# Two more chunks of the output projection as filler in attention, and a final pass over two chunks with its weights in the shared buffers

## The chip, the cores and the metric

The kernel runs on one core of a Trainium2 chip. The metric is the device time of one execution in microseconds (us). TensorE (PE in the profile) multiplies, VectorE (DVE), ScalarE (ACT) and GpSimd (POOL) work elementwise, SyncE (SP) issues most DMAs. Each engine works through its own queue in order.

## What is computed

Two layers of a hybrid block run over 128 context tokens and 512 latent tokens of width 1024. The part that matters here, cut from the reference:

```python
ya = diff_attention(a_q, a_k, a_v, lam)                      # 4 heads, 256 features
yb = gqa_attention(b_q, b_k, b_v).reshape(b, L, W_B)         # 4 heads, 256 features
yc, ssd_state = ssd_mixer(...)                               # 256 features
yd, s5_state = s5_mixer(...)                                 # 256 features
y = jnp.concatenate([ya, yb, yc, yd], axis=-1) @ P['w_out']  # 1024 x 1024
x = x + gate1 * rmsnorm(y, P['g_post1'])
h = rmsnorm(x, P['g_pre2']) * (1.0 + scale2) + shift2
g, v = jnp.split(dwconv(h @ P['w_up'], P['ffn_conv_w'], P['ffn_conv_b']), 2, axis=-1)
x = x + gate2 * rmsnorm((jax.nn.silu(g) * v) @ P['w_down'], P['g_post2'])
```

## The kernel before

Activations lie with features on the 128 partitions and the 642 token columns (512 latent, 2 padding, 128 context) along the free axis. So a vector of 1024 features is 8 tiles, the chunks 0 to 7 of `self.h`. Chunks 0 to 3 hold the outputs of attention, 4 and 5 that of the SSD, 6 and 7 that of the S5. Every number that is multiplied is split into a high and a low part (`hh` and `hl`, `wh` and `wl` in the trace), and a product is three matmuls: high by high, high by low, low by high.

The columns are worked in two spans, `SPANS`: 0 to 256 and 256 to 642. One output tile of `w_out` over one span is, for each chunk, three matmuls of 256 or 386 columns, which accumulate in one PSUM bank; the bank is then copied or added into the SBUF tile `y[m]` (lines 1565 and 1567).

The order of the work follows from priorities: `self.prio(p)` gives the instructions traced in it a number, counting up, and a planner with a model of the chip's times orders each engine's queue by it; a lower number goes first where several are ready. Inside a layer the S5 comes first (0), then its GLU (10000), attention (20000), the SSD (30000), the projections (40000), all plus 100000. What comes later is filler for the gaps of these: the adaLN matmuls of layer 0 (`fill`, 160000 and 161000), then the output projection in three steps: chunks 6 and 7 from `WP[0]` (161000), chunks 0 and 1 from `WP[1]` (162000), and the final pass over chunks 4, 5, 2 and 3 with `PR["wg"]` (165000) for the first span and `PR["norm"]` (300000) for the second.

The SSD and attention run beside each other. Attention has six units; units 0 to 2 fill chunks 0 and 1, units 3 and 4 chunk 2, the last unit chunk 3. A unit handles single tiles of 128 queries: scores on PE into bank `e`, maxima on DVE, exponentials on ACT, then transposes and the products with the values on PE.

The final pass is the part after attention that all else waits for. For each span it sums the squares of `y`, and `norms` makes the norm, the gated residual, the second norm's sums and its scaling (`postnorm`, `rstd`, `prenorm`). The first span's `prenorm` is held back as `self.pending` and run in the middle of the second span's pass (`between`). Then `ffn_first` multiplies the first eight tiles of `w_up`.

Weights come through the pool `wp`, which has two raw buffers `wr` and two pairs `wh`, `wl`. `load_w` loads a tile of 512 KB into `wr`, casts it on ACT to `wh` and subtracts on DVE and POOL in turn for `wl` (lines 96 and 99). With `keep` the pair lies in another pool instead: for the final pass the pool `wo`, with four pairs `kh`, `kl`, opened on the right side behind `x`. `w_out_load(l, k0, nk)` with `nk = 2` makes two loads of two chunks by four output tiles, with `nk = 1` one load of one chunk by eight. `leading`, which `ffn_first` calls, loads the first two `w_up` tiles into `wh`, `wl` of `wp`, the next two by `load_w2` into tiles of the pool `f`, whose space attention holds until its end, and four more into the pool `wx`, which lies where `wo` was.

Of the kernel before, what the change touches and what calls it, by code (L numbers as in the profile page):

```python
# [18 lines left out]
NS = 512  # L19
PO = 514  # L20
SPLIT = 256
WG = (((4, 2), (2, 1), (3, 1)),)
WB = ("pe", "pe")
AHEAD = 1
L0BANKS = "ppvue"
WR = 2
# [47 lines left out]
class K:  # L74
# [1406 lines left out]
    def mixer(self, l, base, fill):  # L1481

        self.qd = {}
        with ExitStack() as left, ExitStack() as early:
            if l == 0:
                self.start()
            self.vec = self.vecs[l]
            self.dbg(f"h{l}", self.h[0][0].bitcast(F32))
            kq = left.enter_context(self.pool(f"kq{l}"))
            at = left.enter_context(self.pool(f"at{l}"))  # L1490
            vt = left.enter_context(self.pool(f"vt{l}"))
            proj = left.enter_context(ExitStack())
            pb = proj.enter_context(self.pool(f"pj{l}"))
            with self.pool(f"ld{l}", bufs=2) as lead, self.prio(base + PR["proj"]):
                raw = self.first_proj(l, pb, lead)
            pc = proj.enter_context(self.pool(f"pc{l}"))
            qk = early.enter_context(self.pool(f"qk{l}", "right"))
            with self.prio(base + PR["proj"]):
                sp = early.enter_context(self.pool(f"s5{l}", "right"))
                raws = {"aq0": raw[0], "ak0": raw[1]}  # L1500
                self.cf = {}
                for op in ORD.split():
                    o, n = op[0], op[1:]
                    if o == "R":
                        self.ropes(qk, int(n))
                    elif o == "V":
                        self.vdt(l, vt)
                    elif o == "P":
                        raws[n] = self.raw_proj(l, pb, n)
                    elif o == "Q":  # L1510
                        self.qk_prep(l, qk, n, raws.pop(n))
                    elif o == "C":
                        self.ssd_proj(l, pb, pc, n)
                    elif o == "Z":
                        self.proj(l, f"cz{n}", self.putcz[int(n)])
                    else:
                        for t in self.cz:
                            self.silu2(self.raw(pb), t, t)
            with self.prio(base + PR["st"]):
                self.ssd_steps(pb)  # L1520
            with self.prio(base + PR["s5"]):
                ys = self.s5(l, sp, pb)
            fill(0, base + PR["f0"])
            with self.prio(base + PR["glu"]):
                self.s5_glu(l, sp, ys)
            early.close()
            yp = self.right.enter_context(self.pool(f"y{l}", "right"))
            with self.pool(f"sd{l}", "right") as sd, self.prio(base + PR["ssd"]):
                self.ssd(l, sd, pb)
            proj.close()  # L1530
            with self.prio(base + PR["attn"]):
                self.attention(l, at, kq)
        y = [yp.tile([P, TW], F32, tag=f"y{c}", name=f"y{c}") for c in range(8)]
        with self.prio(base + WP[0]):
            self.w_out(l, y, self.w_out_load(l, 6, 2))
        fill(1, base + PR["f1"])
        with self.prio(base + WP[1]):
            self.w_out(l, y, self.w_out_load(l, 0, 2))
        return yp, y
# [58 lines left out]
    def run(self):  # L1598
        nc, tc, a, o = self.nc, self.tc, self.a, self.o
        PS = bass.MemoryType.PSUM  # L1600
        self.left0 = ExitStack()
        with self.pool("cp") as self.cp, self.pool("modp", bufs=2) as self.modp, \
                self.pool("hp") as self.hp, self.pool("wp", bufs=2) as self.wp, \
                self.pool("pd", space=PS) as self.psd, \
                tc.tile_pool(name="dp", bufs=2, space=bass.MemoryType.DRAM) as self.dp:
            self.mod, self.vecs, self.s5d = {}, {}, {}
            self.h = []
            for c in range(8):
                self.h.append(tuple(self.hp.tile([P, TW], F32R, tag=f"{q}{c}", name=f"h{q}{c}") for q in "hl"))
                for t in self.h[c]:  # L1610
                    nc.gpsimd.memset(t[:, NS:PO].bitcast(F32), 0.0)
            self.cst = self.cp.tile([P, NCST - 128], F32, tag="cst", name="cst")
            self.identr = self.cp.tile([P, 128], F32R, tag="idr", name="identr")
            xd = a["xT"]
            for l in range(L):
                base = 1000000 * l
                with ExitStack() as self.right:
                    with self.pool(f"pm{l}", space=PS) as self.psm:

                        def fill(i, p):  # L1620
                            if l == 0:
                                with self.prio(p):
                                    self.weave(self.adaln(0, 1 + i, 2 + i, self.wp))
                        yp, y = self.mixer(l, base + 100000, fill)
                        for c in range(8):
                            self.dbg(f"yc{l}{c}", self.h[c][0].bitcast(F32))
                        xp = self.right.enter_context(self.pool(f"x{l}", "right"))
                        fp = self.right.enter_context(self.pool(f"f{l}"))
                        with self.prio(base + PR["norm"]), self.pool(f"wo{l}", "right", 4) as wo:
                            self.x = [xp.tile([P, TW], F32, tag=f"x{c}", name="x") for c in range(8)]  # L1630
                            for c in range(8):
                                nc.sync.dma_start(self.x[c], xd[:, c, :])
                            ws = [sum((self.w_out_load(l, k, n, wo) for k, n in g), []) for g in WG]
                            for gi, (t0, t1) in enumerate(SPANS):
                                st = self.sums("vd"[gi])

                                def put(m):
                                    self.square(fp, st, gi, y[m], m)
                                if gi == 0:
                                    for i, w in enumerate(ws):  # L1640
                                        with self.prio(base + PR["wg"] + 1000 * i):
                                            self.w_out(l, y, w, ((t0, t1),), put if i == len(WG) - 1 else None, WB[i])
                                else:
                                    self.w_out(l, y, sum(ws, []), ((t0, t1),), put, WB[-1])
                                self.norms(fp, gi, st, y, (l, 0), (l, 1))
                        with self.prio(base + PR["first"]):
                            first = self.ffn_first(l, fp, yp)
                    self.dbg(f"xm{l}", self.x[0])
                    last = l == L - 1
                    xt = o["yT"] if last else self.dp.tile([P, 8, TW], F32, tag="xd", name="xd")  # L1650
                    with self.prio(base + 320000), self.pool(f"qb{l}", bufs=2, space=PS) as self.pbig:

                        def tables():
                            if not last:
                                with self.pool(f"t{l + 1}", "right") as tp, self.prio(base + 320300):
                                    self.s5_tables(l + 1, tp, "dd", base + 320300)
                                self.vec = self.vecs[l]

                        def finish(gi, st, y):
                            self.norms(fp, gi, st, y, (l, 1), None if last else (l + 1, 0), xt)  # L1660
                        side = ExitStack()
                        wm = None if last else side.enter_context(self.pool(f"wm{l}", "right"))

                        def other():
                            if not last:
                                yield from self.adaln(l + 1, 0, 3, wm, "vu", 3)
                        self.ffn(l, fp, yp, first, tables, finish, other(), side.close)
                    xd = xt
# [145 lines left out]
```

## Time and profile before

| | us |
|---|---|
| three runs: median | 2218.14 |
| three runs: lowest and highest | 2208.99, 2224.91 |
| the profiled execution | 2229.98 |
| its span, from the first to the last instruction | 2228.2 |

The profiled execution is 11.8 us above the median of the runs. Durations below come from it. In its trace a matmul's duration is longer than the distance to the next one, as matmuls are pipelined: the distance is what counts. In names of tiles `psp` is PSUM bank `p`, `pse` bank `e`, and so on; `kh` and `kl` are the weights of the final pass, of the `w_up` tiles 4 to 7 and of the last `w_down` tiles.

### The profile page before, as it was taken

What the parts mean: (1) busy time and instruction counts of PE and PEld (TensorE: products, weight loads), DVE (VectorE), ACT (ScalarE), POOL (GpSimd) and SP (SyncE); (2) the same over time, 40 slices, a digit from 0 to 9 for tenths busy, and PEclk for the clock granted to TensorE, in tenths of its full rate; (3) what the DMA queues carried; (4) which work ended last, traced back from release to release, by engine and by line L of the source; (5) the groups of instructions that cost most, each with busy time, mean ns of one, the idle gap of its engine ahead of it and who ended that gap; (6) DMA issues with size and microseconds to landing.
All of it is one profiled execution on the core that took longest, in us unless ns stands there. A gap on an engine that the chain in (4) does not pass through costs nothing. (4 is left out here: it accounts for less than half of the span.)

```text
span 2228.2 us, 33233 instructions
## 1 busy us (share of the span) xinstructions
PE 1970.5 (88%) x12812; PEld 1794.6 (81%) x12812; DVE 1234.3 (55%) x2847; ACT 802.3 (36%) x1614; POOL 674.9 (30%) x723
## 2 busy tenths in 40 slices
PE   5996789958889999999998888787787999999997
PEld 2895765646888878899988887776777999999996
DVE  6876885356569567233357576563845641333345
ACT  3423354334344223222334244352533442323231
POOL 3552423111143343122234332323202332222232
PEclk9996789887889999999998878877857999999998
DMA  7464325241214575422233632210102112222221
GB/s 290 134 207 155 114 89 167 84 127 47 67 39 138 159 264 169 131 82 61 88 93 93 217 117 80 84 65 10 59 19 85 39 48 86 71 73 72 80 86 48
DMA packets 93511, 230.29 MB, mean 103 GB/s; under 512 B 17960, under 2 KB 30888, under 8 KB 93352
## 3 DMA queue, kind: packets, MB, share of 16 engines
q1 hardware_dynamic: 82856, 213.46, 30.3%
q10 hardware_dynamic: 10496, 14.71, 1.9%
q8 instruction: 101, 1.65, 0.3%
q14 instruction: 58, 0.48, 0.1%
HBM read 192.21 MB, written 35.92 MB: 102 GB/s over the span
## 5 line engine op out<-in xcount | busy, mean ns | idle before, releaser
L82 PE MATMUL psb<-hh,wh 128*128 128x256 f32 (+1 forms) x1152 | 358.8, 311 | 2.3 <-DVE cv L452 2.3
L82 PE MATMUL psb<-hl,wh 128*128 128x256 f32 (+1 forms) x1152 | 358.0, 311 | 0.0
L82 PE MATMUL psb<-hh,wl 128*128 128x256 f32 (+1 forms) x1152 | 357.1, 310 | 0.0
L99 POOL TENSOR_TENSOR wl<-wr,wh 128x1024 fp32r<-128x1024 f32 (+3 forms) x83 | 182.1, 2194 | 512.2 <-ACT wh L96 488.8
L96 ACT CAST wh<-wr 128x1024 fp32r<-128x1024 f32 (+3 forms) x166 | 160.4, 966 | 420.7 <-PE psb L82 289.2
L82 PEld LDWEIGHTS psb<-hh,wh 128*128 128x128 f32 x1152 | 217.7, 189 | 13.3 <-issue 8.2
L82 PEld LDWEIGHTS psb<-hl,wh 128*128 128x128 f32 x1152 | 218.5, 190 | 3.4 <-issue 3.4
L82 PEld LDWEIGHTS psb<-hh,wl 128*128 128x128 f32 x1152 | 217.8, 189 | 3.4 <-issue 3.4
L82 PE MATMUL psp<-hh,wh 128*128 128x386 f32 (+1 forms) x544 | 182.1, 335 | 29.0 <-ACT wh L96 17.0
L99 DVE TENSOR_TENSOR wl<-wr,wh 128x1024 fp32r<-128x1024 f32 (+3 forms) x83 | 96.8, 1167 | 160.0 <-ACT wh L96 159.7
L82 PE MATMUL psp<-hl,wh 128*128 128x386 f32 (+1 forms) x544 | 177.5, 326 | 0.0
L82 PE MATMUL psp<-hh,wl 128*128 128x256 f32 (+1 forms) x544 | 175.1, 322 | 0.0
L82 PE MATMUL psb<-uh,wh 128*128 128x256 f32 (+1 forms) x544 | 169.7, 312 | 0.0
L82 PE MATMUL psb<-ul,wh 128*128 128x256 f32 (+1 forms) x544 | 169.3, 311 | 0.0
L82 PE MATMUL psb<-uh,wl 128*128 128x256 f32 (+1 forms) x544 | 168.9, 311 | 0.0
L82 PE MATMUL pse<-k,q 96*128 96x128 f32 (+5 forms) x288 | 114.5, 462 | 45.5 <-ACT at_p L1196 18.6
L82 PEld LDWEIGHTS psp<-hh,wh 128*128 128x128 f32 x544 | 109.9, 202 | 34.1 <-ACT wh L96 17.2
L82 PEld LDWEIGHTS pse<-k,q 96*128 96x128 f32 (+2 forms) x288 | 63.0, 237 | 77.4 <-issue 28.8
L1420 POOL TENSOR_TENSOR cv<-cv,cv 128x642 f32<-128x642 f32 x44 | 71.6, 1629 | 170.3 <-DVE cv L452 140.9
L451 DVE SCALAR_TENSOR_TENSOR cv<-psb,vec,cv 128x641 f32<-128x641 f32 x72 | 63.5, 882 | 103.5 <-ACT cv L450 103.5
L82 PEld LDWEIGHTS psp<-hl,wh 128*128 128x128 f32 x544 | 109.4, 201 | 2.3 <-issue 1.0
L82 PEld LDWEIGHTS psp<-hh,wl 128*128 128x128 f32 x544 | 108.5, 200 | 0.9 <-DVE wl L99 0.3
(525 smaller groups left out, 4922.6 us busy)
## 6 DMA issues: line engine op xcount, KB each, us to landing
wm<-in_w_mod SPq DMA_DIRECT2D x96, 512.0 KB
wr<-in_w_up SPq DMA_DIRECT2D x88, 512.0 KB
wr<-in_w_in SPq DMA_DIRECT2D x30, 512.0 KB
wr<-in_w_down SPq DMA_DIRECT2D x32, 384.0 KB
wr<-in_w_down SPq DMA_DIRECT2D x32, 320.0 KB
wr<-in_w_out SPq DMA_DIRECT2D x16, 512.0 KB
s_tb<-s5td SPq DMA_DIRECT2D x8, 992.0 KB
s_to<-s5td SPq DMA_DIRECT2D x8, 768.0 KB
```

The source lines that it names most:

```text
L82: self.nc.tensor.matmul(out, w, x, start=start, stop=stop)
L96: nc.scalar.copy(hv, rv)
L99: e.tensor_sub(lv, rv, hv.bitcast(F32))
L451: nc.vector.scalar_tensor_tensor(out[:, 1:TW], x[:, 0:TW - 1], w[:, 0:1], out[:, 1:TW], op0=ALU.mult, op1=ALU.add)
L1420: G.tensor_mul(cv[0], cv[0], cv[1])
```

## The change

`WG` and the pool `wo` go. Chunks 4 and 5 leave the final pass and become a second filler with priority `WP[0]`, traced behind chunks 6 and 7 and ahead of chunks 0 and 1; their tiles are added into `y`. The final pass covers chunks 2 and 3. Its two weight loads no longer use a pool of their own but the pairs `wh`, `wl` of `wp`, and they get the priority `PR["wg"]` instead of `PR["norm"]`, ahead of the loads of `x`. The first span's pass has `PR["wg"] + 1000`.

```diff
-WG = (((4, 2), (2, 1), (3, 1)),)
-WB = ("pe", "pe")
+WB = "pe"
...
         with self.prio(base + WP[0]):
-            self.w_out(l, y, self.w_out_load(l, 6, 2))
+            for k in (6, 4):
+                self.w_out(l, y, self.w_out_load(l, k, 2))
         fill(1, base + PR["f1"])
...
-                        with self.prio(base + PR["norm"]), self.pool(f"wo{l}", "right", 4) as wo:
+                        with self.prio(base + PR["norm"]):
+                            with self.prio(base + PR["wg"]):
+                                ws = self.w_out_load(l, 2, 1) + self.w_out_load(l, 3, 1)
                             self.x = [xp.tile([P, TW], F32, tag=f"x{c}", name="x") for c in range(8)]
                             for c in range(8):
                                 nc.sync.dma_start(self.x[c], xd[:, c, :])
-                            ws = [sum((self.w_out_load(l, k, n, wo) for k, n in g), []) for g in WG]
                             for gi, (t0, t1) in enumerate(SPANS):
                                 st = self.sums("vd"[gi])
...
-                                if gi == 0:
-                                    for i, w in enumerate(ws):
-                                        with self.prio(base + PR["wg"] + 1000 * i):
-                                            self.w_out(l, y, w, ((t0, t1),), put if i == len(WG) - 1 else None, WB[i])
-                                else:
-                                    self.w_out(l, y, sum(ws, []), ((t0, t1),), put, WB[-1])
+                                with self.prio(base + PR["wg"] + 1000) if gi == 0 else ExitStack():
+                                    self.w_out(l, y, ws, ((t0, t1),), put, WB)
                                 self.norms(fp, gi, st, y, (l, 0), (l, 1))
```

## Rows read from the trace of the kernel before

**Rows 1.** The page, part 1: busy us of each engine, share, instructions

```profile
PE 1970.5 (88%) x12812; PEld 1794.6 (81%) x12812; DVE 1234.3 (55%) x2847; ACT 802.3 (36%) x1614; POOL 674.9 (30%) x723
```

**Rows 2.** Stretches: length; busy PE, PEld, DVE, ACT, POOL (counts); clock, DMA share, GB/s

```profile
460.00:545.00 85.00, 55.23 (x294) 44.13 (x293) 47.95 (x123) 34.83 (x96) 16.88 (x11) 0.78 0.27 82
545.00:582.00 37.00, 33.19 (x162) 27.84 (x162) 14.21 (x37) 12.06 (x36) 0.00 (x0) 0.64 0.22 72
1570.00:1645.00 75.00, 59.51 (x291) 48.61 (x291) 53.46 (x137) 37.78 (x107) 14.34 (x11) 0.70 0.17 58
1645.00:1687.00 42.00, 38.15 (x161) 33.84 (x161) 14.00 (x35) 12.12 (x34) 0.00 (x0) 0.50 0.19 63
```

**Rows 3.** Tile `y`, by form: durations in ns (least, median, most), first and last start

```profile
L1567 DVE TENSOR_TENSOR y<-y,psp x48: 401/480/559, 492.2 to 1713.2; 128x256 f32<-128x256 f32 x24, 128x386 f32<-128x386 f32 x24
L1567 DVE TENSOR_TENSOR y<-y,pse x16: 414/482/558, 585.0 to 1714.5; 128x256 f32<-128x256 f32 x8, 128x386 f32<-128x386 f32 x8
```

**Rows 4.** Timeline of PE, layer 0, early matmuls of the final pass: start, duration

```profile
516.87 0.28 PE L82 MATMUL psp<-hh,kh 128*128 128x256 f32 x1
516.99 0.28 PE L82 MATMUL psp<-hl,kh 128*128 128x256 f32 x1
...
555.67 0.58 PE L82 MATMUL pse<-hh,kh 128*128 128x256 f32 x1
```

**Rows 5.** Timeline of PE, layer 0, final pass to `ffn_first`

```profile
581.93 0.58 PE L82 MATMUL psp<-hh,kh 128*128 128x256 f32 x1 [0.46 <-ACT hh L156]
...
590.67 0.34 PE L82 MATMUL psp<-hh,kh 128*128 128x386 f32 x1
...
600.50 0.61 PE L82 MATMUL psv<-identr,rq_y 128*128 128x128 f32 x4
...
608.39 0.34 PE L82 MATMUL pse<-hh,kl 128*128 128x386 f32 x1
...
621.00 0.58 PE L82 MATMUL psp<-hh,wh 128*128 128x256 f32 x1 [2.41 <-ACT hh L375]
```

**Rows 6.** Chain of work that ended last, layer 1, in order of time

```profile
1660.74 1.92 PE pse L82 x9
...
1667.61 1.92 PE pse L82 x9
...
1686.85 0.58 PE psp L82
...
1706.08 0.46 PE psv L82 x4
```

**Rows 7.** Timeline of DVE and then POOL, layer 0, final pass and norm

```profile
582.72 1.28 DVE L112 TENSOR_TENSOR ul<-wr,uh 128x640 fp32r<-128x640 f32 x2
...
601.15 1.66 DVE L392 SCALAR_TENSOR_TENSOR nt<-y,gpost,psv 128x256 f32<-128x256 f32 x4 [0.77 <-PE psv L82]
...
609.62 0.42 DVE L321 TENSOR_TENSOR nsq<-nsq 128x256 f32<-128x256 f32 x1
...
610.86 1.22 DVE L99 TENSOR_TENSOR kl<-wr,kh 128x1024 fp32r<-128x1024 f32 x1 [0.29 <-ACT kh L96]
612.00 2.63 DVE L318 TENSOR_TENSOR nsq<-nsq 128x256 f32<-128x256 f32 x1
...
611.85 2.50 POOL L99 TENSOR_TENSOR kl<-wr,kh 128x1024 fp32r<-128x1024 f32 x1 [3.00 <-ACT kh L96]
```

**Rows 8.** Timeline of SP and ACT, layer 0: loads of `w_out` and the wait

```profile
466.67 33.72 SPq L89 DMA_DIRECT2D wr<-in_w_out  x6
...
485.75 1.04 ACT L96 CAST wh<-wr 128x1024 fp32r<-128x1024 f32 x1 [18.25 <-DMA wr<-in_w_out]
```

**Rows 9.** Chunks 4, 5, then 1 complete: timeline (layer 0); 4, 5: tile `hl` (layer 1)

```profile
446.54 1.69 DVE L157 TENSOR_TENSOR hl<-cf,hh 128x512 fp32r<-128x512 f32 x4
...
455.12 0.28 DVE L157 TENSOR_TENSOR hl<-psd,hh 128x128 fp32r<-128x128 f32 x1
...
L157 DVE TENSOR_TENSOR hl<-cf,hh x4: 286/486/687, 1566.0 to 1568.8; 128x512 fp32r<-128x512 f32 x2, 128x128 fp32r<-128x128 f32 x2
```

## The prediction

> **What bounds the kernel now.** I read the page first. The reader should see that TensorE (PE) is busy for 88% of the span, with the other engines at 55% and less [rows 1]: a PE matter, but only where PE sets the end. So the second view is the table by stretch around the place of the change, for both layers [rows 2]. In the attention stage behind the SSD, PE is busy 55.2 of 85 us in layer 0 and 59.5 of 75 us in layer 1, DVE 48 and 53.5: no engine is full, waits between engines set the pace. In the tail of attention (its last unit) PE is busy 33.2 of 37 and 38.2 of 42 us at a granted clock of 0.64 and 0.50, and the chain of waits runs over PE without a break; there PE is the bound. The third view is PE's timeline of the final pass [rows 5]. In layer 0 its first span (256 columns) takes 581.93 to 590.67, its second (386 columns) 590.67 to 608.73. Then PE stands until the norm chain gives `ffn_first` its input at 621.00. The second span's pass is cover for that chain, not the bound. So the pass behind attention is worth much less than its matmuls, and the question is what its halves cost where they go.
>
> **How many matmuls move.** Per layer the final pass has 8 tiles x 2 spans x 4 chunks x 3 = 192 matmuls, afterwards 96: 48 of 256 columns, 48 of 386. But the trace shows that 36 of the old ones run before attention ends [rows 4]: 12 from 516.87 (two tiles' chunks 4, 5 in bank p), 6 once chunk 2 is there, 18 in bank e from 555.67 on (two tiles' chunks 4, 5, 2; two groups of nine like that). Layer 1 has the same 36. 60 of the first span's 96 are left for behind attention.
>
> **(a) First span of the final pass: -2.8 us a layer.** Of the new 48, chunk 2's matmuls for the four tiles that have a bank can go early as now, 12; 36 are left instead of 60. A 256-column matmul starts 0.12 us after the last one at full clock (516.87, 516.99 [rows 4]) and 0.213 us at the half level (1.92 us for 9 [rows 6]). 60 x 0.118 = 7.1, so 1.7 of the 8.74 us are the half-clock start; 36 x 0.118 + 1.7 = 5.9. Gain 2.8; bounds 2.8 and 8.74 x 24/60 = 3.5.
>
> **(b) Early matmuls in the tail of attention: -2 us.** Of the 18 in bank e, 12 are of chunks 4 and 5 and go. They run at half clock, and in layer 1 both groups of nine stand in the chain that ends last, 1.92 us each [rows 6]. 12 x 0.213 = 2.6 us at most, 0 if a wait shows up behind them; I take 2, since PE's pieces follow one another there.
>
> **(c) Norm sums get through PE sooner: -3 us.** The first span's column sums and its spread factor are queued on PE among the second span's matmuls: the spread stands at 600.50, 9.8 us into the second span [rows 5], some 56 matmuls of 0.176 us; in layer 1 the same spread is reached over pieces of the second span in the chain [rows 6]. With groups of 6 instead of 12, 28 of them go: 4.9 us. The other bound is 0, as the place is fixed by when DVE has the sums. I take 3.
>
> **(d) Splits of the first `w_up` tiles move into the norm chain: +5 us.** This is the hidden price. Pool `wo` goes, so chunks 2 and 3 sit in the only two `wh`/`wl` pairs of `wp` until the second span's last matmul. `leading` splits its first two tiles into these same pairs, and both `wr` buffers hold their raw data meanwhile, so tiles 2 and 3 can't even be loaded. Before, tiles 0 and 1 were split during attention and tiles 2 and 3 at 582 (DVE's two subtractions for one tile take 1.28 us at 582.72), only tiles 4 to 7 in the chain [rows 7]. Afterwards all eight are split between the end of the pass and `ffn_first`. What one batch costs there can be read: at 610.86 DVE spends 1.22 us on tile 4, and the sum of squares behind it takes 2.63 us, where its sisters take 0.42, while POOL's 2.50 us on tile 5 run beside it: 1.22 + 2.21 = 3.4. From the spread on DVE hardly rests (postnorm begins at 601.15), so tiles 0 and 1 cost another 3.4 and tiles 2 and 3 2 x 1.28 = 2.6: 6.0, less one `y` addition of 0.54 that is now over earlier. I take 5; bounds 0 (if the splits fall ahead of the spread) and 6. The loads themselves I take as hidden: the first matmul of tile 4 is needed 4 x 24 x 0.118 = 11 us behind the first of tile 0, and the cover for them is `ffn_first` itself.
> [...]
>
> **(e) Attention stage: +4 us.** 96 matmuls of chunks 4 and 5 come in, 12 of them were there already: 36 x 0.118 + 48 x 0.176 = 12.7 us of PE at full clock, and 16 more additions into `y` of 0.48 us on DVE [rows 3], 7.7 us (64 such additions become 96 in all). They can start at once: `hl` of the SSD is complete at 448 in layer 0 and 1569 in layer 1, chunk 1 at 455 in layer 0 [rows 9]. They are queued ahead of `w_out(0, 2)`, which waits for the `wh` pairs and for `y`, and behind them on PE, DVE and ACT stand the scores, maxima and exponentials of attention. PE has 29.8 us idle in layer 0, but 18.25 of these are one wait: ACT, in order, stands at the split of the `w_out` weights until 485.75 for a load issued behind 466.67 [rows 8]. I expect this wait again, since the new chunk's loads take the same place behind the adaLN loads. So some 12 us are usable, 15.5 in layer 1, against 12.7 needed: it fits barely. Nothing on the path would be 0; everything on it 12.7. Were the matmuls evenly spread (about a fifth of the time), some 40 PE steps of attention would each meet half a group of six (0.5 us) one time in five, 4 us; I take 4.
>
> No other DMA is added (eight `w_out` loads a layer before and after), the queue of SP keeps its order, and the `x` loads move behind two weight loads that are issued long before; I cost that at nothing.
>
> **Sum.** -2.8 - 2 - 3 + 5 + 4 = +1.2 us a layer, +2.4 for two. The profiled execution took 2229.98 us (span 2228.2), so 2232.4 by it; it lies 11.8 above the median of the runs, so on the median 2218.14 + 2.4 = 2220.5. I forecast 2220: no change.
>
> **Rivals.** *Cover for free* (faster): the fillers fall into idle time wholly (e = 0), and the splits ahead of the spread (d = 0), with b = 2.6 and c = 4.9: -10.3 a layer, 2218 - 20.6 = 2197. For it: idle time is there in both stages. Against it: it needs all four at once.
> *The stage is full* (slower): once the added 12.7 us exceed the idle time that attention's waits can spare, each matmul is on the path: e = 12.7, the rest as above: +9.9 a layer, 2238. For it: 12 us usable against 12.7 in layer 0. Against it: layer 1 has 15.5.
> *The order slips*: `w_out(0, 2)` is delayed by the chunk ahead of it into the last unit, where PE is the bound at half clock. If its last two tiles (24 matmuls) fall there, that is 24 x 0.213 = 5 us a layer more, 2230. Against it: in layer 0 its bank is free for the final pass at 516.87 [rows 4], 28 us before that tail.
> [...]
> [...]
>
> **How the numbers follow.** Chances: forecast 0.57, own range 2209 to 2231; cover for free 0.14; stage full 0.17; order slips 0.08; clock 0.04. About 1% is what a measurement of this kernel can tell from no change; the three runs before spread over 0.7%. Faster by over 1% (below 2196) is the clock, or free cover and a little more: 0.10. Slower by over 1% (above 2240) needs the full stage and a wait besides: 0.12. Within: 0.78. Range for 8 in 10: 2195 to 2241.
>
> **What would show it.** In the profile after: (a) attention's end to the start of the second span near 6 us instead of 8.7; (b) six instead of eighteen matmuls in bank e before it; (c) spread some 7 us behind the second span's start; (d) splits of eight `w_up` tiles between the pass and `ffn_first`, and PE's idle stretch there grown from 12 to about 23 us; (e) the stretch from the SSD's end to the last unit some 4 us longer in each layer, the 18 us wait of ACT still there. The forecast is wrong if that wait vanishes or a second one like it appears, or if the stage stretches by more than 10 us.

## The result, and the profile after

The changed kernel takes 2192.66 us (median of 4, 2190.0 to 2200.85) against 2217.89 (2208.99 to 2224.91): a ratio of 0.9895, 95% interval 0.985 to 0.9939. Measured a second time, beside the experiments, the same kernel gave 0.9884 (0.9841 to 0.9927). I had forecast no change, 2220, with 2195 as the lower end of the range. The profiled execution took 2191.5 us (span 2189.7), against 2229.98 before. The latter lies 11.8 above its median, so of the 38 us between the two traces some 12 are that one execution's.

The first view is a table of stretches in the two traces. Its marks are the ends of the last writes into tiles `hl` (S5's output, the SSD's output, each unit of attention, the norm's output).

| stretch (us) | layer 0 before | after | layer 1 before | after |
|---|---|---|---|---|
| S5's output to SSD's output | 121.6 | 115.0 | 117.1 | 117.2 |
| SSD to the end of the last unit but one | 97.6 | **77.3** | 75.8 | 75.6 |
| last unit of attention | 37.0 | 36.3 | 42.7 | 38.6 |
| final pass and norm chain | 80.6 | 78.3 | 77.8 | 76.0 |
| S5 stage of layer 1 (ahead of its SSD) | | | 240.1 | 239.9 |

27 of the 38 us are gone in layer 0 between S5 and the last unit but one; layer 1, with the same moved matmuls, gives 6. That speaks against the moved matmuls as what pays; the experiments test it.

Page, part 1, after (answers [rows 1]): PE's share is one point higher, its busy time 14 us lower.

```profile
PE 1956.1 (89%) x12812; PEld 1786.6 (82%) x12812; DVE 1245.6 (57%) x2879; ACT 802.4 (37%) x1614; POOL 676.4 (31%) x723
```

Busy time by stretch (columns as in [rows 2]). First the kernel before, from the SSD's end in layer 0, and its last unit; then after: the same two stretches of layer 0, and both in layer 1.

```profile
448.00:546.00 98.00, 65.20 (x345) 49.22 (x345) 56.28 (x148) 39.69 (x110) 17.89 (x12) 0.80 0.32 94
546.00:583.00 37.00, 33.19 (x165) 28.41 (x165) 14.21 (x37) 12.85 (x36) 0.00 (x0) 0.64 0.22 72
```
```profile
440.00:517.00 77.00, 71.03 (x359) 47.74 (x358) 47.68 (x137) 32.83 (x103) 7.74 (x8) 0.83 0.37 118
517.00:554.00 37.00, 36.76 (x253) 33.67 (x253) 24.03 (x60) 15.14 (x36) 4.14 (x2) 0.93 0.40 129
...
1537.00:1612.00 75.00, 66.42 (x380) 58.67 (x378) 58.03 (x153) 35.33 (x105) 12.45 (x10) 0.84 0.14 44
1612.00:1651.00 39.00, 35.01 (x152) 30.78 (x152) 15.17 (x38) 12.07 (x33) 0.00 (x0) 0.54 0.20 68
```

In layer 0 PE rests 6 of 77 us after, against 33 of 98 before. And the last unit now holds 253 matmuls instead of 165 in the same 37 us, at a granted clock of 0.93 instead of 0.64.

Timeline of SP after, layer 0 (answers [rows 8]):

```profile
378.94 4.16 SPq L88 DMA_DIRECT2D wr<-in_w_out  x2
403.70 18.15 SPq L226 DMA_DIRECT2D wm<-in_w_mod  x2
446.27 0.54 SPq L1182 DMA_DIRECT2D q<-d_bq  x1
449.80 0.52 SPq L1174 DMA_DIRECT2D k<-d_bk  x1
450.38 1.39 SPq L1175 DMA_DIRECT2D k<-d_bk  x1
451.82 0.65 SPq L1182 DMA_DIRECT2D q<-d_bq  x1
469.53 34.59 SPq L226 DMA_DIRECT2D wm<-in_w_mod  x14
510.52 14.26 SPq L88 DMA_DIRECT2D wr<-in_w_out  x4
```

The loads for chunks 4, 5 are issued at 378.94, before the 16 adaLN loads (`wm`) of `fill(1)` and 67 us before the q and k loads. Before, all these 16 ran first, then q and k, and the next `w_out` loads stood right behind these, at 466.67 [rows 8]. ACT's casts of weights from 375 to 540, grouped, with what ended its idle time before them:

```profile
L95 ACT CAST wh<-wr x7: 1037/1046/1050, 375.3 to 534.1; 128x1024 fp32r<-128x1024 f32 x7
...
  DMA wr<-in_w_out: 4.9, 2
```

The one wait of 18.25 us [rows 8] is gone: 4.9 us in two are left.

### The profile page after: what moved, and what is told of

It is laid out like the page before. It is cut to its first block, busy times and chain, and to the rows that moved or that the text cites. A ratio compares the mean times of both kernels' runs of the same rounds, so it can differ in the third digit from the quotient of the medians.

```text
span 2189.7 us, 33260 instructions
## 1 busy us (share of the span) xinstructions
PE 1956.1 (89%) x12812; PEld 1786.6 (82%) x12812; DVE 1245.6 (57%) x2879; ACT 802.4 (37%) x1614; POOL 676.4 (31%) x723
## 4 chain that ended last, share of the span: by engine, by line
PE 67%; DVE 15%; DMA 9%; ACT 3%; issue 2%; POOL 2%; SPq 1%; ACTq 0%; POOLq 0%; DVEq 0%
PE psb L81 34%; PE psp L81 12%; PE psd L81 7%; PE pse L81 6%; PE psv L81 5%; DMA s_tb<-s5td 2%; DMA wm<-in_w_mod 1%; DVE nt L391 1%; PE psu L1209 1%; DMA wr<-in_w_down 1%; DVE x L394 1%; DMA ck<-in_cache_ak 1%; DVE wl L98 1%; DMA q<-d_bq 1%; DVE at_s L1279 1%
## 5 line engine op out<-in xcount | busy, mean ns | idle before, releaser
L98 POOL TENSOR_TENSOR wl<-wr,wh 128x1024 fp32r<-128x1024 f32 (+3 forms) x87 | 192.3, 2211 | 502.7 <-ACT wh L95 451.6
L95 ACT CAST wh<-wr 128x1024 fp32r<-128x1024 f32 (+3 forms) x174 | 168.6, 970 | 417.9 <-PE psb L81 283.4
L81 PE MATMUL psp<-hh,wh 128*128 128x386 f32 (+1 forms) x640 | 215.3, 337 | 10.7 <-ACT hh L374 7.8
L81 PE MATMUL psp<-hl,wh 128*128 128x386 f32 (+1 forms) x640 | 209.8, 328 | 0.1
L81 PE MATMUL psp<-hh,wl 128*128 128x386 f32 (+1 forms) x640 | 207.0, 324 | 0.3 <-POOL wl L98 0.3
L81 PE MATMUL pse<-k,q 96*128 96x128 f32 (+5 forms) x288 | 107.1, 436 | 44.6 <-ACT at_p L1195 15.1
L81 PEld LDWEIGHTS psp<-hh,wh 128*128 128x128 f32 x640 | 129.0, 202 | 17.4 <-ACT hh L374 8.8
L81 PEld LDWEIGHTS psp<-hl,wh 128*128 128x128 f32 x640 | 129.3, 202 | 2.6 <-issue 1.1
L81 PEld LDWEIGHTS psp<-hh,wl 128*128 128x128 f32 x640 | 128.6, 201 | 1.4 <-issue 0.5
```

The lines of the kernel that those rows point to most:

```text
L81: self.nc.tensor.matmul(out, w, x, start=start, stop=stop)
L95: nc.scalar.copy(hv, rv)
L98: e.tensor_sub(lv, rv, hv.bitcast(F32))
```

## The experiments

Theories. *Order*: layer 0 gains because the adaLN filler is held behind the new chunks, and so the order of loads on SP changes. *Cover*: it gains because the chunks' matmuls fill idle time. One table holds the stretches of the profiled kernels, one execution of each; a ratio is the time against the kernel before, measured beside the run. Where an expectation is in us, the ratio times the 2218 of the first comparison stands beside it.

| kernel (us) | SSD, layer 0 | to last unit but one | last unit | S5 stage, layer 1 | last unit, layer 1 |
|---|---|---|---|---|---|
| before | 121.6 | 97.6 | 37.0 | 240.1 | 42.7 |
| after | 115.0 | 77.3 | 36.3 | 239.9 | 38.6 |
| after_again | 115.6 | 80.8 | 35.7 | 244.0 | 40.2 |
| fill_between | 120.5 | 98.1 | 38.5 | 250.2 | 38.5 |
| fill_last | 116.5 | 78.9 | 48.1 | 245.5 | 41.2 |
| loads_early | 118.3 | 94.6 | 42.7 | 251.7 | 28.6 |
| layer1_only | 120.6 | 101.4 | 31.6 | 242.1 | 38.6 |
| qk_rows | 120.9 | 89.6 | 31.7 | 225.5 | 42.7 |
| fill_between_rows | 121.7 | 86.9 | 38.5 | 244.8 | 38.7 |
| after_qk_rows | 113.7 | 82.6 | 34.1 | 232.7 | 38.6 |
| after_qk_rows2 | 114.4 | 83.1 | 36.8 | 230.7 | 38.5 |
| all_rows | 114.9 | 74.5 | 40.2 | 203.4 | 38.6 |
| own_pairs | 114.2 | 83.0 | 35.8 | 242.4 | 40.2 |
| rows_own_pairs | 114.7 | 82.4 | 38.9 | 237.3 | 38.6 |

**fill_between: the changed kernel with the filler where I had assumed it.**

```
         with self.prio(base + WP[0]):
-            for k in (6, 4):
-                self.w_out(l, y, self.w_out_load(l, k, 2))
+            self.w_out(l, y, self.w_out_load(l, 6, 2))
         fill(1, base + PR["f1"])
+        with self.prio(base + WP[0] + 500):
+            self.w_out(l, y, self.w_out_load(l, 4, 2))
```

> The changed kernel with one thing put back: the adaLN filler is called between chunks 6, 7 and chunks 4, 5, as my forecast had assumed it would run, so that the 16 adaLN weight loads and the q and k loads of the last attention heads stand ahead of the loads for chunks 4, 5 on SP again. All matmuls of chunks 4, 5 stay in the attention stage and the final pass keeps two chunks. Order theory (layer 0 gains because the filler is held behind the new chunk, which moves the w_out loads ahead of the q and k loads): ACT waits 15 to 18 us for w_out weights in layer 0 again, the stage from the SSD's end to the last unit is back near 90 us from 69, and the time is 2207 to 2215. Cover theory (layer 0 gains because the chunks' matmuls fill idle time): no such wait decides, 2190 to 2197.

Measured: 2231.55, ratio 1.0024 (0.9987 to 1.006): the gain is gone. By the ratio that is 2223, above both of my ranges. The waits of its attention stage in layer 0 (engine, line, waited for: us in total, times, longest) and its SP timeline:

```profile
ACT wh L95 <- DMA wr<-in_w_out: 18.7, 2, 18.4
...
PE psp L81 <- ACT wh L95: 15.9, 1, 15.9
```
```profile
467.60 0.52 SPq L1182 DMA_DIRECT2D q<-d_bq  x1
468.21 24.09 SPq L88 DMA_DIRECT2D wr<-in_w_out  x4
```

The load for chunks 4, 5 stands right behind q and k, and the wait is back with 18.4 us. Order is borne out; cover is not. But the sum of the run is not all order: layer 0, from S5's output to the norm's end, is 1 us longer than before, layer 1 behind its S5 stage some 4 us shorter, and 10 us more come from the S5 stage of layer 1. There the planner wrote another order on SP, with four q loads at 1232.15 ahead of S5's table, whose load is issued at 1249.55, 34 us into the stage; before, it goes out at 1222.07, 10 us in. That this order is the reason isn't shown: in loads_early that stage is as long (251.7) with the table's load 10 us in.

**after_again, layer1_only: the change again, and in layer 1 alone** (layer 0 keeps the code of before).

> The changed kernel itself, beside the others on one chip. Every theory: ratio 0.985 to 0.994 to before, as the first comparison gave.

> The change in layer 1 alone; layer 0 is that of the kernel before. Layer 1 has no adaLN filler and no late w_out load. Order theory: only the small terms of the forecast are left, layer 1 from the SSD's end to the end of the norm chain gets 3 to 8 us shorter and layer 0 keeps its wait of 18 us, ratio 0.996 to 0.999. Cover theory (the two layers gain alike): half of the gain, ratio 0.993 to 0.996.

Measured: 2197.45, ratio 0.9884 (0.9841 to 0.9927), and 2220.96, ratio 0.9984 (0.9954 to 1.0014). Layer 1 alone gives nothing that can be told from no change, as order expects and cover (0.993 to 0.996) does not; its trace is 3 us shorter from the SSD to the norm's end. Its layer 0 is that of the kernel before, and shows how far one code's stretches lie apart: 101.4 and 31.6 us where the trace of before has 97.6 and 37.0.

**fill_last: the kernel before with the filler called behind chunks 0, 1.** No matmul leaves the final pass.

```
-        fill(1, base + PR["f1"])
         with self.prio(base + WP[1]):
             self.w_out(l, y, self.w_out_load(l, 0, 2))
+        fill(1, base + PR["f1"])
```

> The kernel before with one thing moved: the adaLN filler is called behind w_out of chunks 0, 1 instead of ahead of it. No matmul moves between the attention stage and the final pass, which keeps four chunks. Order theory: the loads for chunks 0, 1 come ahead of the q and k loads, ACT's wait of 18.25 us is gone, the SSD ends some 4 us sooner, 2192 to 2202. Cover theory: 2214 to 2222, as before.

Measured: 2207.48, ratio 0.993 (0.9899 to 0.996), by the ratio 2202: the upper end of the range I gave for order, and well below cover's. The loads for chunks 0, 1 are issued at 382.14, ahead of the 16 adaLN loads from 403.42 on. The SSD and the stage behind it are as short as in the changed kernel, 116.5 and 78.9. But the last unit takes 48.1:

```profile
520.00:568.00 48.00, 42.97 (x201) 32.88 (x200) 21.21 (x44) 19.38 (x42) 7.16 (x3) 0.61 0.44 142
```

201 matmuls at a clock of 0.61: the end of the filler (its last matmul starts at 533.27) now lies in the stretch where PE is the bound. 24 us are gained ahead, 11 given back.

**loads_early: the kernel before, loads for chunks 0, 1 ahead of the filler, their matmuls behind it.**

```
             self.w_out(l, y, self.w_out_load(l, 6, 2))
+            w01 = self.w_out_load(l, 0, 2)
         fill(1, base + PR["f1"])
         with self.prio(base + WP[1]):
-            self.w_out(l, y, self.w_out_load(l, 0, 2))
+            self.w_out(l, y, w01)
```

> The kernel before with only the loads (and splits) for chunks 0, 1 issued right behind those of chunks 6, 7; the filler is still called ahead of the matmuls of chunks 0, 1. Order theory in its narrow form (the wait of ACT for the late load is what costs): the wait is gone, the SSD still shares PE with the filler, 2196 to 2205. Order theory in its wide form (the filler in the SSD's time is what costs): 2210 to 2218, the wait gone but a new one in its place. Cover theory: 2214 to 2222.

Measured: 2229.77, ratio 1.0039 (1.0003 to 1.0075), above every range I gave. A miss for the narrow form: ACT's wait is gone, but PE has one as long in its place. SP's timeline and the waits:

```profile
459.26 0.51 SPq L1183 DMA_DIRECT2D q<-d_bq  x1
459.87 7.74 SPq L227 DMA_DIRECT2D wm<-in_w_mod  x2
```
```profile
PE psp L82 <- DMA wm<-in_w_mod: 21.0, 5, 17.6
```

Now two adaLN loads stand behind q and k, and PE stands 17.6 us for one of them. So it isn't the `w_out` load that is slow: in before (18.25 us), in fill_between (18.4) and here the wait is for what stands right behind the q and k loads. The sum of this run also holds an S5 stage of layer 1 that is 12 us longer and a last unit there that is 14 us shorter; the last section has the latter.

**qk_rows: the kernel before, q and k rows issued by blocks.**

```
-                nc.sync.dma_start(q[i].bitcast(F32), self.qd[f"bq{u}"][0:2, r])
+                for j in range(2):
+                    nc.sync.dma_start(q[i][64 * j:64 * j + 64].bitcast(F32), self.qd[f"bq{u}"][j, r])
```

The same is done to the load of k1.

> The kernel before with one thing changed: the three 128-row loads of q and k for the last attention heads, which read two blocks of 64 rows each, are issued as two loads of 64 rows. Same bytes, same place on SP, all else as before. In the trace of before the 448 rows of these loads drain at some 20 a us of 104 ns each from 462 to 484, and the first w_out weights behind them land at 485; the one load of a single block of 64 rows went out in a burst. Theory (whatever weight load stands right behind the q and k loads is late by what they take, and an in-order engine stands on it): the rows drain in under 8 us, ACT's wait of 18.25 us falls under 6, the stage is 12 to 18 us shorter, ratio 0.992 to 0.995 to before. Rival (the w_out loads are slow for their own sake, or the q and k rows are bound by something else): rows drain as slowly, ratio 0.998 to 1.002.

Measured: 2200.04, ratio 0.9882 (0.9818 to 0.9946), without moving any work: as much as the change, and more than I had expected, but not where I had expected it. The stage behind the SSD is 8.0 us shorter than before, where I had said 12 to 18. The last unit is 5.3 us shorter, which needs no split, as it is as short in layer1_only. 15 us are gone from the S5 stage of layer 1, where more q and k rows of this kind are loaded; what became shorter there was not followed. Counted in the traces' DMA packets, the 448 rows of 2568 bytes take from 461.7 to 483.8 before (20 a us at 104 ns each; by these two numbers some two transfers at a time, an estimate) and from 464.1 to 469.6 here (81 a us). Of the 512 packets of the first two `w_out` loads before, 448 had started by 479.2; then none did for 3.7 us, and the last 64, an eighth, started from 482.9 to 486.5, as the rows ran out. The longest wait of ACT for these loads is now:

```profile
ACT kh L96 <- DMA wr<-in_w_out: 6.2, 1, 6.2
```

Why rows of two blocks drain at a quarter of the rate, and why an eighth of the packets of the loads behind them comes only as they run out, was not shown.

**after_qk_rows, fill_between_rows, all_rows: the same split on the other kernels.** The last splits also the loads of the a heads, three blocks of 32 rows.

> The changed kernel with the same split of the q and k loads. There the adaLN loads behind the q and k loads are issued only when the rows are gone, so the order theory expects the stage as it is: ratio 0.987 to 0.991 to before, within 0.3% of the changed kernel beside it. If these rows also hold up the attention of the last heads, the stage of 69 us shortens by up to 10 us and the ratio is 0.983 to 0.987.

> The changed kernel with the q and k loads of the b heads split into blocks of 64 rows, a second time, beside the two below. Every theory: ratio 0.978 to 0.987 to before.

> fill_between (the change, with the adaLN filler back ahead of chunks 4, 5) with the q and k loads of the b heads split into blocks of 64 rows. It differs from after_qk_rows only in the filler's place, and from qk_rows only by the moved matmuls. If the filler's place cost only through the late load: ACT's wait is under 7 us and the ratio is that of after_qk_rows, 0.980 to 0.985. If the filler also costs by sharing the SSD's time (121 against 115 us from S5 to the SSD's end): 0.984 to 0.990, and the gain of the moved matmuls by themselves, against 0.988 of qk_rows, is 0.3% or less.

> As after_qk_rows, and the loads of q and k for the a heads, which read three blocks of 32 rows each, are issued as three loads of 32 rows too. If rows of a load of several blocks drain slowly wherever they stand and what is behind them is late, it gains a little more: ratio 0.975 to 0.981. If nothing that is awaited stands behind those loads, or the two more issues per load on SP cost as much: within 0.3% of after_qk_rows.

Measured: after_qk_rows 2184.55 and 2186.32, ratios 0.9825 (0.9784 to 0.9867) and 0.9823 (0.9785 to 0.9861), lower than order expected (0.987 to 0.991); its stage behind the SSD is no shorter than after's, and most of the gain lies again in the S5 stage of layer 1. fill_between_rows 2211.26, ratio 0.9942 (0.9909 to 0.9975): worse than both my cases. ACT's wait is under 3 us there, and the stage is 11 us shorter than in fill_between (86.9 against 98.1), but against after_qk_rows the SSD is 121.7 instead of 113.7, the stage 86.9 instead of 82.6, and the S5 stage of layer 1, in fill_between's other order on SP, 12 us longer. So the filler's place costs beyond the wait. The SSD takes 118.3 to 121.7 in the six kernels of the table that run 100 or more of the filler's 128 matmuls in its time, and 113.7 to 116.5 in the eight that run 64 or fewer there: some 5 us.

all_rows: 2157.38, ratio **0.9698** (0.9654 to 0.9742), more than I had expected, and faster than both kernels. Where four loads of three blocks stand alone, in layer 0, their 384 rows drain at 28 a us in after (307.9 to 321.7) and at 66 here (296.2 to 302.0). The gain is in the S5 stage of layer 1, where the a heads' loads stand among those of S5's tables and of the projection weights. That stage by busy time, in after and then in all_rows:

```profile
1180.00:1420.00 240.00, 202.13 (x1324) 189.81 (x1323) 146.52 (x324) 94.45 (x218) 75.03 (x87) 0.84 0.39 125
```
```profile
1177.00:1381.00 204.00, 189.25 (x1342) 179.50 (x1341) 142.37 (x324) 92.34 (x222) 77.79 (x93) 0.93 0.45 141
```

The first q loads of that stage on SP's timeline, in after and in all_rows:

```profile
1203.58 3.12 SPq L1166 DMA_DIRECT2D q<-d_aq  x4
```
```profile
1205.30 8.85 SPq L1168 DMA_DIRECT2D q<-d_aq  x12
```

Three times as many issues, and the stage is 36 us shorter (29 against after_qk_rows); PE's mean clock in it is 0.93 instead of 0.84. Which of the waits in it went first was not followed.

**own_pairs, rows_own_pairs: step (d) by itself.** The changed kernel, and after_qk_rows, with two pairs of buffers of their own for chunks 2, 3.

```
-                        with self.prio(base + PR["norm"]):
+                        with self.prio(base + PR["norm"]), self.pool(f"wo{l}", "right", 2) as wo:
                             with self.prio(base + PR["wg"]):
-                                ws = self.w_out_load(l, 2, 1) + self.w_out_load(l, 3, 1)
+                                ws = self.w_out_load(l, 2, 1, wo) + self.w_out_load(l, 3, 1, wo)
```

> The changed kernel, but the weights of chunks 2, 3 get two pairs of buffers of their own instead of the two pairs that the first w_up tiles also use, so that tiles 0 and 1 of w_up can be split during attention again. Step (d) of the forecast: the stretch from the norm's spread to the first product of the feed-forward part, 22.6 us in layer 0 and 25.3 in layer 1, gets 2 to 5 us shorter in each layer, 2183 to 2189. If the splits hide in the norm chain: 2191 to 2195.

> As after_qk_rows, with the two pairs of buffers of own_pairs for chunks 2, 3. Step (d) of the forecast, now beside the same kernel without it: norm chain 2 to 4 us shorter per layer, ratio 0.002 to 0.004 below after_qk_rows. If the earlier loads and splits of w_up cost as much in the attention stage (its last stage but one took 75.5 and 73.9 us in own_pairs against 68.9 and 67.7): the same within 0.2%.

Measured: 2204.56, ratio 0.9911 (0.9886 to 0.9937), and 2191.46, 0.9837 (0.9794 to 0.988). The final pass and norm chain are 2.8 and 2.5 us shorter (75.5, 73.5) than after, and 75.9, 74.3 in the second. The stretch that I had named, from the spread to the first product of the feed-forward part, is back at 21.2 from 25.3 in layer 1 in both: there the price of (d) is real. In layer 0 it is 23.7, 1 us longer than after's 22.7, so what is gained there comes behind the first product. The whole is not faster than without it, a miss for both ranges of own_pairs (2198 by the ratio), and within 0.2% of after_qk_rows2 beside it for the second; other stretches that the planner rearranged are longer (in own_pairs layer 1's stage before the last unit is 81.8 against 75.6).

## Why the prediction was wrong

**What bounds, and (a): right in the mechanism; (c): mis-sized.** Timeline of PE after, layer 0 (answers [rows 5]):

```profile
552.90 0.38 PE L81 MATMUL psp<-hh,wh 128*128 128x256 f32 x1 [0.21 <-ACT hh L155]
...
558.51 0.34 PE L81 MATMUL psp<-hh,wh 128*128 128x386 f32 x1
...
567.45 0.38 PE L81 MATMUL psv<-identr,rq_y 128*128 128x128 f32 x2
...
590.15 0.58 PE L81 MATMUL psp<-hh,wh 128*128 128x256 f32 x1 [3.48 <-ACT hh L374]
```

The first span takes 5.6 us (said: 5.9, from 8.74). The spread stands 8.9 us behind the second span's start (said: some 7, from 9.8): (c) is 0.9 in both layers, not 3. I had 28 of the matmuls ahead of it go; but it stands behind all 48 of the second span's pass, and before behind 53 of 96. Its input is ready at 565.43, 6.9 us into the second span (before: 6.4), so DVE's sums come no sooner, and it waits 2 us more for its place in PE's queue. In layer 1 (a) and (c) together are 4.9 us, in layer 0 4.0, where I had 5.8.

**(b)** -2 forecast. Six matmuls in bank e instead of eighteen, as said, in both layers. In layer 1 the last unit is 4.1 us shorter and the chain shows no group of nine in bank e; [rows 6] had two of 1.92. In layer 0, where other work came into the last unit, it is 0.7 shorter.

**(d)** +5 forecast. All eight splits fall into the chain, and PE's rest there is 22.1 us (568.05 to 590.15), where I had said about 23. Timeline of DVE and then POOL after (answers [rows 7]):

```profile
568.51 1.22 DVE L98 TENSOR_TENSOR wl<-wr,wh 128x1024 fp32r<-128x1024 f32 x1
...
575.38 2.34 DVE L111 TENSOR_TENSOR ul<-wr,uh 128x640 fp32r<-128x640 f32 x2
...
578.84 1.28 DVE L111 TENSOR_TENSOR ul<-wr,uh 128x640 fp32r<-128x640 f32 x2
...
569.01 2.92 POOL L98 TENSOR_TENSOR wl<-wr,wh 128x1024 fp32r<-128x1024 f32 x1 [3.58 <-ACT wh L95]
```

The two subtractions for one tile into `ul` take 2.34 us beside POOL, which works from 575.31 to 578.30, and 1.28 for the next tile, with POOL at rest. From the spread to the first product of the feed-forward part it is 22.7 us instead of 20.5 in layer 0, 25.3 instead of 21.2 in layer 1: +2.2 and +4.1. In layer 1 a load stands in the chain that ended last (start, us), ahead of POOL's split:

```profile
1675.54 3.43 DMA wr<-in_w_up
...
1680.12 2.40 POOL kl L98
```

I had taken these loads as hidden behind `ffn_first`. This one is not, and with buffers of their own for chunks 2, 3 (own_pairs) layer 1 gets its 4 us back. Layer 0 does not, so what its 2.2 us are stays open.

**(e), the matmuls**: +4 forecast. They are free. Layer 1's stage is 75.6 against 75.8 with 84 more matmuls, and layer 0's in fill_between, wait and all, 98.1 against 97.6. The additions stand as forecast [rows 3]:

```profile
L1567 DVE TENSOR_TENSOR y<-y,psp x80: 395/478/558, 443.5 to 1663.5; 128x256 f32<-128x256 f32 x40, 128x386 f32<-128x386 f32 x40
L1567 DVE TENSOR_TENSOR y<-y,pse x16: 412/486/558, 555.4 to 1664.6; 128x256 f32<-128x256 f32 x8, 128x386 f32<-128x386 f32 x8
```

**(e), the wait: the step that failed.** I wrote: "I expect this wait again, since the new chunk's loads take the same place behind the adaLN loads", and that the queue of SP keeps its order. Neither holds. The code calls `w_out` of chunks 4, 5 ahead of `fill(1)`. I had read the priorities, by which the filler (161000) could overtake them. But both take the two buffers `wr` of pool `wp` (the tiles `wm` have that tag) and both write bank p, and in the trace after they got these in the order of the code. fill_last shows it too: there the loads for chunks 0, 1, with the later number 162000, go ahead of the filler. So the chunks' loads got the buffers at 378.94; the filler's could be issued only as the chunks were split, at 403.70 and 421.5, and its matmuls went on behind the chunks' in bank p, from 468.4 to 509.4 instead of 420.4 to 463.5. That did three things in layer 0. No awaited load stands behind q and k any more: their rows drain as slowly as before, from 447.6 to 469.0, but nothing is issued behind them until 469.53, and ACT's wait of 18.25 us is gone. The SSD shares PE with 64 of the filler's matmuls instead of 104, and is 6.6 us shorter. And the loads for chunks 0, 1 slip to 510.52, their matmuls into the last unit.

The stage is 20 us shorter. The wait is worth 8 to 12 of them, by the kernels in which split rows take it away or cut it: the stage is 8.0 us shorter in qk_rows than before, 11.8 shorter than in layer1_only with the same layer 0, and 11.2 shorter in fill_between_rows than in fill_between. How the rest divides between the filler that came into the stage and the matmuls of chunks 0, 1 that left it was not separated.

fill_between is the kernel that my sum describes, and it gave 1.0024, that is 2223 on the median I worked from (2215 to 2231), where I had 2220. That is in part luck: its layer 0 is 1 us longer than before, as the sum says, but its layer 1 is 4 us shorter, where (e) was 4 us too high and (b) 2 too small, and 10 us come from the S5 stage of layer 1, which no term holds. I had even named the sign, "wrong if that wait vanishes", and had given it no chance and no price: 18.25 us stood in the rows.

**The rivals.** *Cover for free* had a time close to the result (2197) by luck, with the wrong cause: e was 0 as it said, but d was not, and the wait isn't in it. *The stage is full* fell. *The order slips* took place: the last unit of layer 0 holds 253 instead of 165 matmuls. It took 36.3 us instead of 37.0, at a clock of 0.93 instead of 0.64. Against the 31.6 of layer1_only, where that unit has its old work at 0.83, it may have cost up to 5 us. The chance that I called clock, 0.04, was for tails of attention that get shorter at a higher granted clock. I had kept it small for two tails of equal length at different clocks: from the first group in bank e to the end, 26.3 us in layer 0 (555.67 to 581.93, clock 0.69) and 26.1 in layer 1 (1660.74 to 1686.85, 0.50). That reading was wrong. The two tails don't hold the same work: layer 0's has 130 matmuls, layer 1's 108. That more matmuls in a stretch raise its clock is not shown either: the last unit of layer 0 had 253 at 0.93 in after and 201 at 0.61 in fill_last, and 165 or 166 at 0.50 in loads_early, 0.64 in before and 0.82 in qk_rows. See the last section for two stretches that are alike.

## What to carry to other kernels

When a filler is moved past another, list what the two share (buffers of one tag, a bank, a queue) and take the order from there; in these runs a priority decided only between instructions that could both go. A long wait in the profile is a term of the sum of its own: ask what it would take to make it vanish, and price that, even for a change that is not aimed at it. And when an awaited load is late, look at what was issued ahead of it, and at how many rows a microsecond that drains, before moving the load: splitting the q and k loads alone gave as much as this change, and the change with all splits nearly three times as much.

## What the runs showed of the hardware

Loads of 128 rows in two blocks of 64 drained at 20 rows a us (before), the same rows as loads of one block at 81 (qk_rows); of the two loads behind the former an eighth of the packets, 64 of 512, came only as the rows ran out, and an engine that needed such a load stood 17.6 (loads_early), 18.25 (before) and 18.4 us (fill_between) for it.

One stretch differed by 14 us with its granted clock. The last unit of layer 1, with the same 165 matmuls, in the kernel before (from [rows 2], here 1 us longer) and in loads_early:

```profile
1645.00:1688.00 43.00, 39.15 (x165) 34.84 (x166) 15.00 (x37) 13.12 (x36) 0.00 (x0) 0.50 0.18 62
```
```profile
1657.00:1686.00 29.00, 24.86 (x165) 21.50 (x166) 14.98 (x38) 13.01 (x36) 0.00 (x0) 0.85 0.27 91
```

It takes 29 us at 0.85 instead of 43 at 0.50; in before every 2 us of it from 1645 to 1687 stand at 0.50. It goes with how far executions of one program lie apart here: 63 executions of the kernel before, beside the experiments, took 2207.6 (mean clock 0.902) to 2239.6 us (0.886), with a correlation of -0.92 between time and clock. So a difference of a few us in one stretch of one trace can be the clock's. What sets the clock of such a stretch was not tried.
